# The last tile of an average pool: one load of 64 KB a partition and one whole sum, in place of two column halves

## The chip, the cores and the metric

The kernel runs on one core of a Trainium2 chip. The core has several engines that run side by side and wait for each other through semaphores: TensorE (PE, not used here), VectorE (DVE), ScalarE (ACT), GpSimd (POOL) and SyncE (SP, which here only issues DMAs). Data moves between the chip's HBM and the core's SBUF memory (128 partitions) through 16 DMA engines. The metric is the device time of one execution in microseconds (us); a span, in a profile, is the time from the first to the last event of the program.

## The reference

The input is `x`, float32, of shape 32 x 256 x 4096. Each row of 4096 values is cut into 256 windows of 16 and each window is averaged. The output is 32 x 256 x 256, float32.

```
for i in range(output_size):
    start = int(i * length / output_size)
    end = int((i + 1) * length / output_size)
    result[:, :, i] = np.mean(x[:, :, start:end], axis=-1)
```

So 134.22 MB are read, 8.39 MB are written, and there is about one addition for each value read.

## The kernel before, in words

The 32 x 256 = 8192 rows are cut into 16 tiles of 512 rows. A tile puts four rows (R = 4) on each of the 128 partitions: 4 x 4096 values, 64 KB a partition, 8.39 MB in all. The first fifteen tiles are taken from the first 7680 rows, of which each partition holds 60 in a row, and the last tile (`x_last`, `o_last`) from the last 512 rows. Results of the first fifteen tiles gather in one buffer, `res_many` (60 KB a partition), those of the last in `res_last` (4 KB a partition).

Input tiles come from a pool of two buffers, both named `xin`, so a tile's load waits until the work on the tile two before it has finished with the buffer. All loads are issued by SP, and run in the order of their issue on one DMA queue (q1 in the profile).

`pooled` (L62 to L75) does the work of one stretch of `n` windows, in four instructions:

- POOL (L66) takes the second half of the windows and adds the right 8 values of each onto the left 8, in place;
- VectorE (L69) sums the 16 values of each window of the first half;
- VectorE (L70) sums the 8 values that POOL left of each window of the second half, and so waits for POOL;
- ScalarE (L73) multiplies all `n` results by 1/16, and waits for both sums.

Each engine works through its instructions in the order of the code. In the loop over the first fifteen tiles `pooled` is called once a tile, on 1024 windows a partition. (A clearing of 1536 columns of the second buffer at L80 holds back the second load a little at the start.)

The last tile is handled apart. Its buffer is loaded by two DMAs (L88 to L92), each of half of the columns: 32 KB a partition, 512 windows. Then `pooled` is called on each half. Both halves' results go into `res_last`.

Stores are issued by ScalarE (L57 to L60) and share a second DMA queue (q10), on which they run in the order of issue. There are three: `res_many` in one transfer of 7.86 MB (L93), which stands in the code behind the loads of the last tile and ahead of its work, so that ScalarE issues it after the fifteenth tile's multiplication; and at the end `res_last` in two transfers, of 120 partitions and of 8 (L97). They count on a semaphore of their own, `stored`, for which SP waits at the end (L103).

Of the kernel before, what the change touches and what calls it, by code (L numbers as in the profile page):

```python
# [1 line left out]

# [4 lines left out]


@with_exitstack
def kernel(  # L10
    ctx: ExitStack,
    tc: tile.TileContext,
    x: bass.AP,
    output_size: int,
    out: bass.AP,
):

    nc = tc.nc
    F32 = mybir.dt.float32
    X = mybir.AxisListType.X

    batch, channels, length = x.shape
    ob, oc, olen = out.shape
    assert ob == batch and oc == channels and olen == output_size
    assert length % output_size == 0
    window = length // output_size  # L30
    hw = window // 2
    inv_w = 1.0 / float(window)

    P = nc.NUM_PARTITIONS
    R = 4
    rows = batch * channels
    assert rows % (P * R) == 0
    ntiles = rows // (P * R)
    many = (ntiles - 1) * R
    cells = R * output_size  # L40
    m = cells // 2
    cols = R * length

    xr = x.rearrange("b c l -> (b c) l")
    orow = out.rearrange("b c o -> (b c) o")
    x_many = xr[0 : P * many, :].rearrange("(p r) l -> p (r l)", p=P, r=many)
    o_many = orow[0 : P * many, :].rearrange("(p r) o -> p (r o)", p=P, r=many)
    x_last = xr[P * many :, :].rearrange("(p r) l -> p (r l)", p=P, r=R)
    o_last = orow[P * many :, :].rearrange("(p r) o -> p (r o)", p=P, r=R)

    res_many = nc.alloc_sbuf_tensor("res_many", [P, (ntiles - 1) * cells], F32, align_bytes=256)
    res_last = nc.alloc_sbuf_tensor("res_last", [P, cells], F32, align_bytes=256)
    inpool = ctx.enter_context(tc.tile_pool(name="inpool", bufs=2))

    stored = nc.alloc_semaphore("stored")

    def store(out, in_):  # L57
        ins = nc.scalar.dma_start(out=out, in_=in_)
        tc.no_tile_sem_insts.add(ins.ins.name)
        ins.then_inc(stored, 16)  # L60

    def pooled(xin, res, base, n):  # L62


        k = n // 2
        nc.gpsimd.tensor_add(  # L66
            out=xin[:, k:n, 0:hw], in0=xin[:, k:n, 0:hw], in1=xin[:, k:n, hw:window]
        )
        nc.vector.reduce_sum(out=res[:, base : base + k], in_=xin[:, 0:k, :], axis=X)  # L69
        nc.vector.reduce_sum(  # L70
            out=res[:, base + k : base + n], in_=xin[:, k:n, 0:hw], axis=X
        )
        nc.scalar.mul(  # L73
            out=res[:, base : base + n], in_=res[:, base : base + n], mul=inv_w
        )  # L75

    for t in range(ntiles - 1):
        xbuf = inpool.tile([P, cols], F32, name="xin")
        if t == 1:
            nc.vector.memset(xbuf[:, 0:1536], 0.0)  # L80
        nc.sync.dma_start(out=xbuf, in_=x_many[:, t * cols : (t + 1) * cols])
        pooled(xbuf.rearrange("p (o w) -> p o w", w=window), res_many, t * cells, cells)

    half = cols // 2
    xbuf = inpool.tile([P, cols], F32, name="xin")
    for h in range(2):  # L88
        nc.sync.dma_start(
            out=xbuf[:, h * half : (h + 1) * half],  # L90
            in_=x_last[:, h * half : (h + 1) * half],
        )  # L92
    store(o_many, res_many[:, :])  # L93
    for h in range(2):
        xin = xbuf[:, h * half : (h + 1) * half].rearrange("p (o w) -> p o w", w=window)
        pooled(xin, res_last, h * m, m)
    for lo, hi in ((0, 120), (120, P)):  # L97
        store(o_last[lo:hi, :], res_last[lo:hi, :])

    ctx.pop_all().close()  # L100
    tc.close()
    tc.compile()  # L102
    nc.sync.wait_ge(stored, 48)  # L103
    nc.sync.sem_clear(stored)


# [1 line left out]
_INS = ['x', 'output_size']  # L108
_OUTS = [((32, 256, 256), 'float32')]

_NUMBERS = {'output_size': 256}


# [26 lines left out]
```

## Time and profile before

| | us |
|---|---|
| median of 3 runs | 333.52 (333.38 to 333.53) |
| the profiled execution | 333.36 |
| its span | 332.1 |
| VectorE busy | 211.1 |
| GpSimd busy | 139.9 |
| ScalarE busy | 18.4 |
| DMA: bytes read, written | 134.22 MB, 8.39 MB |
| DMA: mean rate over the span | 429 GB/s |

The profile names an instruction by its line in the code, its engine, its operation and what it writes and reads (`res_many<-xin`), with the shape as partitions x elements. Under "L66", then, stand the POOL additions, under "L69" and "L70" the two sums, under "L73" the multiplications. A line of the timeline gives the start in us from the beginning of the span, the duration, the instruction, and in brackets how long the engine had been idle before it and what ended the wait. "ACTq" and "SPq" are the instructions that issue DMAs. The chain that ended last is read backwards from the program's last work: each step is what released the next one. In the 40-slice row of the DMA engines a 9 means that they were busy for 90% of the slice or more. Below the page, the trace holds a record of each DMA packet (queue, size, start and end); a packet here is what one DMA engine moves for one partition, 65,536 bytes for a whole tile and 32,768 for a half, or the 4-byte write with which it reports that its share of a transfer is done. A transfer over 128 partitions gives each of the 16 DMA engines eight data packets and one such completion write.

### The profile page before, as it was taken

How to read it: one execution, taken by the hardware profiler on the slowest of the kernel's cores; microseconds unless marked ns; L12 is line 12 of the kernel's file. 1: busy time of each engine (PE TensorE's matmuls, PEld its weight loads, DVE VectorE, ACT ScalarE, POOL GpSimd, SP SyncE). 2: the span in 40 equal slices, each digit the busy share in tenths (PEclk: the TensorE clock that was granted, in tenths of full speed). 3: DMA queues.
4: the chain of work that ended last, by engine and by line, in shares of the span. 5: the costliest groups of instructions: out<-in, count | busy, mean ns of one | idle time of the engine just before them, and what ended most of it. 6: DMA issues, size and time to landing. Idle time of an engine off the chain costs nothing.

```text
span 332.1 us, 167 instructions
## 1 busy us (share of the span) xinstructions
DVE 211.1 (64%) x35; ACT 18.4 (6%) x18; POOL 139.9 (42%) x21
## 2 busy tenths in 40 slices
DVE  1029396592939669293966929396693929569770
ACT  1000101001010100101010010101000010100100
POOL 0028091542809154270916427090642709068050
DMA  9898999989898998989899998989899898989997
GB/s 379 379 497 387 482 403 411 474 379 505 379 497 387 458 426 379 505 379 497 387 482 403 395 489 379 505 379 497 387 450 434 379 505 379 497 383 430 442 466 307
DMA packets 2743, 142.61 MB, mean 429 GB/s; under 512 B 311, under 2 KB 311, under 8 KB 439
## 3 DMA queue, kind: packets, MB, share of 16 engines
q1 hardware_dynamic: 2448, 134.22, 93.6%
q10 hardware_dynamic: 295, 8.39, 5.9%
HBM read 134.22 MB, written 8.39 MB: 429 GB/s over the span
## 4 chain that ended last, share of the span: by engine, by line
DMA 62%; POOL 20%; DVE 10%; issue 3%; POOLq 1%; ACT 0%
DMA xin<-in_x_dram 62%; POOL xin L66 20%; DVE res_many L70 9%; POOLq L102 1%; DVE res_last L70 1%; DVE xin L80 0%; ACT res_last L73 0%; POOLq L66 0%
## 5 line engine op out<-in xcount | busy, mean ns | idle before, releaser
L66 POOL TENSOR_TENSOR xin<-xin 128x4096 f32<-128x4096 f32 (+1 forms) x17 | 139.7, 8216 | 179.7 <-DMA xin<-in_x_dram 179.7
L69 DVE TENSOR_REDUCE res_many<-xin 128x512 f32<-128x8192 f32 x15 | 130.3, 8686 | 105.2 <-DMA xin<-in_x_dram 105.2
L70 DVE TENSOR_REDUCE res_many<-xin 128x512 f32<-128x4096 f32 x15 | 66.3, 4419 | 2.4 <-POOL xin L66 2.3
L73 ACT ACTIVATE res_many<-res_many 128x1024 f32<-128x1024 f32 x15 | 15.8, 1056 | 289.9 <-DVE res_many L70 289.9
L69 DVE TENSOR_REDUCE res_last<-xin 128x256 f32<-128x4096 f32 x2 | 8.8, 4414 | 2.1 <-DMA xin<-in_x_dram 2.1
L70 DVE TENSOR_REDUCE res_last<-xin 128x256 f32<-128x2048 f32 x2 | 4.6, 2280 | 0.1
L80 DVE MEMSET xin<- 128x1536 f32 x1 | 1.3, 1338 | 1.1 <-PEq L121 1.1
L73 ACT ACTIVATE res_last<-res_last 128x512 f32<-128x512 f32 x2 | 1.3, 629 | 13.7 <-DVE res_last L70 13.7
L73 ACT ACT_TABLE_LOAD x1 | 1.3, 1283 | 0.7 <-PEq L121 0.7
L121 POOL MEMSET const-float32-0.0<- 128x1 f32 x1 | 0.1, 98 | 0.2 <-issue 0.2
L121 POOL MEMSET const-bfloat16-1.0<- 128x1 bf16 x1 | 0.1, 101 | 0.0
L121 POOL MEMSET const-uint8-127<- 128x1 uint8 x1 | 0.1, 101 | 0.0
L121 POOL MEMSET const-float32-1.0<- 128x1 f32 x1 | 0.1, 98 | 0.0
## 6 DMA issues: line engine op xcount, KB each, us to landing
xin<-in_x_dram SPq DMA_DIRECT2D x2, 4096.0 KB, 21.6
out_dram<-res_many ACTq DMA_DIRECT2D x1, 7680.0 KB
out_dram<-res_last ACTq DMA_DIRECT2D x1, 480.0 KB
xin<-in_x_dram SPq DMA_DIRECT2D x15, 25.3
out_dram<-res_last ACTq DMA_DIRECT2D x1, 32.0 KB
```

The lines of the kernel that those rows point to most:

```text
L66: nc.gpsimd.tensor_add(out=xin[:, k:n, 0:hw], in0=xin[:, k:n, 0:hw], in1=xin[:, k:n, hw:window])
L69: nc.vector.reduce_sum(out=res[:, base : base + k], in_=xin[:, 0:k, :], axis=X)
L70: nc.vector.reduce_sum(out=res[:, base + k : base + n], in_=xin[:, k:n, 0:hw], axis=X)
L73: nc.scalar.mul(out=res[:, base : base + n], in_=res[:, base : base + n], mul=inv_w)
L80: nc.vector.memset(xbuf[:, 0:1536], 0.0)
L102: tc.compile()
L121: nc = _bacc.Bacc("TRN2", target_bir_lowering=False, num_devices=1)
```

## The change

The two DMAs of the last tile become one, of 64 KB a partition, and `pooled` is called once on the whole tile, 1024 windows a partition, as for the other fifteen. The constant `m` goes, since nothing uses it any more. Stores are as before, in the same order.

```
-    m = cells // 2
...
-    half = cols // 2
     xbuf = inpool.tile([P, cols], F32, name="xin")
-    for h in range(2):
-        nc.sync.dma_start(
-            out=xbuf[:, h * half : (h + 1) * half],
-            in_=x_last[:, h * half : (h + 1) * half],
-        )
+    nc.sync.dma_start(out=xbuf, in_=x_last)
     store(o_many, res_many[:, :])
-    for h in range(2):
-        xin = xbuf[:, h * half : (h + 1) * half].rearrange("p (o w) -> p o w", w=window)
-        pooled(xin, res_last, h * m, m)
+    pooled(xbuf.rearrange("p (o w) -> p o w", w=window), res_last, 0, cells)
     for lo, hi in ((0, 120), (120, P)):
         store(o_last[lo:hi, :], res_last[lo:hi, :])
```

On the engines the instructions of the last tile fall from two to one for the load, from two to one for POOL's addition, from four to two for VectorE's sums and from two to one for ScalarE's multiplication, each of twice the size. All other instructions stand in the same order as before.

## The prediction

> **What bounds the kernel now.** I read the page's totals first, then the chain that ended last, then the last 40 us of the timeline, and last the trace's packet records, which give start and end of every DMA packet. Their clock was laid on the timeline's by the last reduction (319.81 us).
>
> ```profile
> DVE 211.1 (64%) x35; ACT 18.4 (6%) x18; POOL 139.9 (42%) x21
> ...
> DMA  9898999989898998989899998989899898989997
> q1 hardware_dynamic: 2448, 134.22, 93.6%
> q10 hardware_dynamic: 295, 8.39, 5.9%
> ```
>
> The 16 DMA engines are busy in every slice, 99.5% over the two queues (q1 loads, q10 stores), while VectorE is busy 64% of the span. Bytes set the time: a compute change costs only where it leaves the DMA engines without work. That can only be at the end, so I look there.
>
> ```profile
> 307.68 7.61 issue
> 315.28 4.50 POOLq L102
> 319.78 0.02 issue
> 319.81 2.30 DVE res_last L70
> 322.10 0.02 issue
> 322.12 0.63 ACT res_last L73
> ```
>
> The chain stops at 322.75, though the span is 332.06: what follows is stores. That the chain runs through compute here doesn't make compute the bound. The timeline shows what lies beside it:
>
> ```profile
> 293.38 8.69 DVE L69 TENSOR_REDUCE res_many<-xin 128x512 f32<-128x8192 f32 x1 [6.04 <-DMA xin<-in_x_dram]
> 293.49 8.72 POOL L66 TENSOR_TENSOR xin<-xin 128x4096 f32<-128x4096 f32 x1 [10.60 <-DMA xin<-in_x_dram]
> 302.24 4.42 DVE L70 TENSOR_REDUCE res_many<-xin 128x512 f32<-128x4096 f32 x1 [0.17 <-POOL xin L66]
> ...
> 306.69 1.06 ACT L73 ACTIVATE res_many<-res_many 128x1024 f32<-128x1024 f32 x1 [18.26 <-DVE res_many L70]
> 307.78 0.38 ACTq L58 DMA_DIRECT2D out_dram<-res_many  x1
> ...
> 315.27 4.42 DVE L69 TENSOR_REDUCE res_last<-xin 128x256 f32<-128x4096 f32 x1 [2.10 <-DMA xin<-in_x_dram]
> 315.32 4.45 POOL L66 TENSOR_TENSOR xin<-xin 128x2048 f32<-128x2048 f32 x1 [7.64 <-DMA xin<-in_x_dram]
> ...
> 322.78 1.04 ACTq L58 DMA_DIRECT2D out_dram<-res_last  x2
> ```
>
> The big store (7.86 MB) is issued at 307.78, the last half lands at 315.27, the small stores (0.52 MB) are issued from 322.78 on the same queue. The packet records tell the rest. The last load's data packets end at 311.9 to 312.6 on the 16 engines. On 15 of them a 61,440-byte packet of the big store (2.27 us) comes next, and the load's 4-byte completion write only behind it, at 314.2 to 314.9: that is why the half lands at 315.27. The big store's packets end at 330.03 to 330.35 on those 15 engines (330.73 on the sixteenth), and the small stores' 4 KB packets follow without a gap to 331.60; the last completion comes at 332.02.
>
> ```profile
> 322.80:330.00 7.20, 0.00 (x0) 0.00 (x0) 0.00 (x0) 1.00 0.94 410
> 330.00:332.06 2.06, 0.00 (x0) 0.00 (x0) 0.00 (x0) 1.00 0.63 255
> ```
>
> In these windows (columns: length, DVE, ACT, POOL busy, clock, DMA share, GB/s) no engine computes for 9 us, and the DMA engines work at 0.94 until 330. So the small stores sit in their queue from 322.78 to 330.03, 7.25 us: that slack is what the change draws on.
>
> **The change, part by part.**
>
> Issue and transfer. SP issues one DMA for two, 0.33 us for 0.81 us, both at 287.37 behind the same wait, with 5 us of the tile before still to land: hidden, worth nothing. The bytes are the same; eight packets of 64 KB an engine (2.417 us each) stand for sixteen of 32 KB (1.213 each), 19.34 for 19.41 us: -0.07 us. The earlier landing of the first half (303.1) is gone.
>
> Work taken away before 315 us. POOL's add at 303.22, DVE's 4.41 + 2.27 from 306.57 and ACT's 0.63 at 313.21 vanish from under the transfer. Nothing waits for them but the second half's work, which started at the landing. On ACT the order stays: fifteenth multiply, big store, then the last tile's multiply; so the big store is issued at 307.78 as before.
>
> Landing. Queue states at 311.9 to 312.6 are the same except for packet size, so I keep 315.27. The bounds: 313.0 if the completion write goes first (312.62 + 0.38 from write to landing), 317.5 if one more store packet (2.27) gets in.
>
> Work after the landing. This is now a whole tile, for which the fifteenth tile is the template: landing 293.38, POOL 8.72, reduction from 302.24, ACT at 306.69, a store issued right behind at 307.78. Landing to issue is 14.40 us. In halves it was 315.27 to 322.78, 7.51. So the small stores are issued at 315.27 + 14.40 = 329.67, 6.89 us later. POOL's add alone is 8.72 - 4.45 = 4.27 of it, the second reduction 4.42 - 2.29 = 2.13, ACT 0.43; rounding and hand-over are the rest. DVE's first reduction (8.69 for 4.42) stays beside POOL's.
>
> What hides it. 6.89 us against 7.25 us in the queue looks free, but an issue isn't a packet. How long an engine takes from issue to useful work on an idle queue, the trace shows once: the first load, issued at 0.74, has its first packets start at 1.73 to 2.42 (0.99 to 1.68 later) and end 1.47 to 2.52 later than issue plus the steady 2.42, median 1.9. The other row is the big store, whose first packet starts 4.13 us after issue, but behind load packets. The engines are idle by 330.4 here, so the first load is nearest; a transfer over 15 engines ends with a late one, so I take 2.0, with 1.0 and 4.1 as ends.
>
> The sum: 329.67 + 2.0 + 8 packets of 0.16 (1.28) + 0.42 (last packet 331.60 to last completion 332.02) + 0.04 to the end of the span = 333.41, against 332.06: **+1.35 us**. The second small store is issued 0.43 later and has one packet an engine (0.16) behind the first's eight: covered. With 1.0 us it is +0.35, with 4.13 us +3.5.
>
> The Trainium skill (DMA: Bandwidth & Descriptors, Latency and other measured facts) states about 600 ns to the first byte on this kind of queue; by that figure packets could start at 330.27, as the big store ends, and the sum would be about 332.0, no change. No engine of the first load did it in under 0.99.
>
> **The base.** The profiled execution took 333.36 us with a span of 332.1; the median of the runs shown is 333.52, 0.16 above. I add the difference to the median: 333.52 + 1.35 = 334.9, rounded down to 334.8 for the 0.07 of the packets. Within 0.2% (0.67 us) is what a measurement can't tell from no change.
>
> **The rivals.**
>
> 1. No change: the completion write goes ahead of the store. For it: the big store was issued at 307.78; with the first load's 0.99 to 1.68 it was ready by 308.8 to 309.5, yet each engine ran one or two more 32 KB packets (from 309.3 and 310.6) before the store's. So an engine seems to pick work ahead. If it does so by number of packets, then with 64 KB packets the completion write is picked before the store is there. Against: picked by bytes or time, the order stays, and one engine of 16 behind a store packet is enough. Price: landing 313.0, issue 327.4, first packet by 329.9 even at 2.5 us, before 330.03: hidden, 333.5. It decides from a landing below about 313.7. The Trainium skill (same page, Queues, rings and completion order) says that an engine drains a whole packet of about 9 to 17 descriptors from one ring before it switches; a share of eight data descriptors and one completion write would then not be broken, and this rival would be the forecast. The trace disagrees on 15 of 16 engines, with a store packet between the eighth and the completion. Chance 0.26.
>
> 2. No change though the landing stays: the small stores start within 1.0 us. +0.35, 333.8. For it: the first load's fastest engine; against: 15 of its 16 ended their first packet 1.66 or more late. Chance 0.07.
>
> 3. Slower still: the store's first packet gets in before the load's eighth, landing 317.5, or the start takes the 4.1 of the big store: +3.5, 337.0. Against the first: at 309.3 to 310.0 every engine took a load packet. Chance 0.06.
>
> That two packets' worth of overhead make it faster: the 0.07 and what the dropped instructions free come nowhere near 0.67. Chance 0.02.
>
> **How the numbers follow.** The forecast (landing kept, start between 1.3 and 2.8 us, +0.7 to +2.1) has 0.59; its own range is 334.2 to 335.7. Slower: 0.59 + 0.06 = 0.65; same: 0.26 + 0.07 = 0.33; faster 0.02. The range takes in rival 1 down to 333.3 and reaches to 335.9, leaving out rival 3 and the far end of the start.
>
> **What would show it.** In the profile after: POOL's sixteenth add near 315.3 with 8.7 us, the last reduction to about 328.5, the small stores' issue near 329.7, and a gap in the DMA engines between 330.4 and 331.7. A first reduction near 313 means rival 1. I'm wrong if the landing moves by 2 us or the store starts much faster or slower than 2 us.

## The result, and the profile after

The changed kernel takes 334.49 us (median of 8 runs, 334.25 to 334.81); the kernel before, beside it, 333.49 us (333.35 to 333.62). The ratio is 1.003, with a 95% interval of 1.0020 to 1.0041: slower by 1.0 us, between 0.7 and 1.4. The forecast was 334.8 and slower by 1.3.

The profiled execution took 334.56 us with a span of 333.2. First its page (totals, queues):

```profile
span 333.2 us, 162 instructions
...
DVE 211.0 (63%) x33; ACT 18.2 (5%) x17; POOL 139.7 (42%) x20
...
DMA  9898989989898989999898989899898989899997
...
q1 hardware_dynamic: 2304, 134.22, 93.2%
q10 hardware_dynamic: 295, 8.39, 6.0%
```

The work is the same to 0.1 to 0.2 us on each engine, and so are the bytes; q1 has 144 records fewer, since the last load has half as many data packets and completion writes. Nothing that is added up here shows where 1 us went. The timeline of the end does:

```profile
293.11 8.69 DVE L68 TENSOR_REDUCE res_many<-xin 128x512 f32<-128x8192 f32 x1 [6.03 <-DMA xin<-in_x_dram]
...
307.51 0.38 ACTq L57 DMA_DIRECT2D out_dram<-res_many  x1
314.90 8.69 DVE L68 TENSOR_REDUCE res_last<-xin 128x512 f32<-128x8192 f32 x1 [8.50 <-DMA xin<-in_x_dram]
315.01 8.72 POOL L65 TENSOR_TENSOR xin<-xin 128x4096 f32<-128x4096 f32 x1 [13.07 <-DMA xin<-in_x_dram]
323.76 4.42 DVE L69 TENSOR_REDUCE res_last<-xin 128x512 f32<-128x4096 f32 x1 [0.18 <-POOL xin L65]
328.21 1.06 ACT L72 ACTIVATE res_last<-res_last 128x1024 f32<-128x1024 f32 x1 [20.73 <-DVE res_last L69]
329.30 0.90 ACTq L57 DMA_DIRECT2D out_dram<-res_last  x2
```

(Line numbers are one to eight lower than before, because lines have gone.) This execution is 0.27 us ahead of the one of before already at the fifteenth tile (293.11 against 293.38). The last tile lands at 314.90 (315.27 before), and the small stores are issued 14.40 us later, at 329.30 (322.78 before). The end of the chain says the same: one wait of 27.76 us for the load, then the tile's work end to end (the piece called `POOLq L94` covers POOL's addition).

```profile
287.11 27.76 DMA xin<-in_x_dram
...
314.98 8.76 POOLq L94
...
323.76 4.43 DVE res_last L69
...
328.21 1.06 ACT res_last L72
```

The packet records show the rest. The big store's packets end at 329.93 to 330.35, nearly as before. The first 4 KB packets of the small stores start at 330.13, 0.83 us after the issue, but 51 of the 128, nearly all of them among the first 64, take more than 0.2 us, about 0.3 on average, where all took 0.159 before. The last one ends at 332.85 (331.60 before), and the last completion comes at 333.21 (332.02). Windows over that second show it (the columns are length, busy DVE, ACT and POOL with their counts, clock, DMA share, GB/s); first the kernel before, then the changed one:

```profile
330.00:331.00 1.00, 0.00 (x0) 0.00 (x0) 0.00 (x0) 1.00 0.85 348
331.00:332.00 1.00, 0.00 (x0) 0.00 (x0) 0.00 (x0) 1.00 0.44 176
```

```profile
330.00:331.00 1.00, 0.00 (x0) 0.00 (x0) 0.00 (x0) 1.00 0.76 172
331.00:332.00 1.00, 0.00 (x0) 0.00 (x0) 0.00 (x0) 1.00 0.86 279
332.00:333.20 1.20, 0.00 (x0) 0.00 (x0) 0.00 (x0) 1.00 0.16 62
```

In the first microsecond after the big store the DMA engines move half of what they moved before, and so the small stores run on into 332 and 333.

### The profile page after: what moved, and what is told of

Its sections match the earlier page's. It is cut to its first block, busy times and chain, and to the rows that moved or that the text cites. A ratio compares the mean times of both kernels' runs of the same rounds, so it can differ in the third digit from the quotient of the medians.

```text
span 333.2 us, 162 instructions
## 1 busy us (share of the span) xinstructions
DVE 211.0 (63%) x33; ACT 18.2 (5%) x17; POOL 139.7 (42%) x20
## 4 chain that ended last, share of the span: by engine, by line
DMA 66%; POOL 18%; DVE 11%; POOLq 3%; issue 0%; ACT 0%
DMA xin<-in_x_dram 66%; POOL xin L65 18%; DVE res_many L69 9%; POOLq L94 3%; DVE res_last L69 1%; DVE xin L79 0%; ACT res_last L72 0%; POOLq L65 0%
## 5 line engine op out<-in xcount | busy, mean ns | idle before, releaser
L65 POOL TENSOR_TENSOR xin<-xin 128x4096 f32<-128x4096 f32 x16 | 139.5, 8717 | 183.8 <-DMA xin<-in_x_dram 183.8
L68 DVE TENSOR_REDUCE res_last<-xin 128x512 f32<-128x8192 f32 x1 | 8.7, 8686 | 8.5 <-DMA xin<-in_x_dram 8.5
L69 DVE TENSOR_REDUCE res_last<-xin 128x512 f32<-128x4096 f32 x1 | 4.4, 4419 | 0.2 <-POOL xin L65 0.2
L72 ACT ACTIVATE res_last<-res_last 128x1024 f32<-128x1024 f32 x1 | 1.1, 1056 | 20.7 <-DVE res_last L69 20.7
```

What stands on the lines that cost most here:

```text
L65: nc.gpsimd.tensor_add(out=xin[:, k:n, 0:hw], in0=xin[:, k:n, 0:hw], in1=xin[:, k:n, hw:window])
L69: nc.vector.reduce_sum(out=res[:, base + k : base + n], in_=xin[:, k:n, 0:hw], axis=X)
L72: nc.scalar.mul(out=res[:, base : base + n], in_=res[:, base : base + n], mul=inv_w)
```

## The experiments

My theory: all the loss is the later issue of the small stores. That issue comes 14.40 us after a landing which itself waits behind a packet of the big store, and it costs only as far as it comes too late to be hidden by the big store. Rivals: the 64 KB transfer costs something by itself; the whole sums do; or the late landing isn't due to the store's packet.

**One part at a time: one load, two sums.** The kernel before, with the new load only:

```
-    for h in range(2):
-        nc.sync.dma_start(
-            out=xbuf[:, h * half : (h + 1) * half],
-            in_=x_last[:, h * half : (h + 1) * half],
-        )
+    nc.sync.dma_start(out=xbuf, in_=x_last)
```

> The load of the last tile is one transfer of 64 KB a partition, the sums stay in two halves. My theory (the loss is the later issue of the small stores, and comes from all data landing at once): landing near 315 as in both kernels, then VectorE works 4.41 + 2.27 + 4.41 + 2.27 = 13.4 us and ScalarE 0.63, so the small stores are issued 14.1 to 14.2 us after the landing, about 0.2 us sooner than in the changed kernel (14.40), and the time is 334.2 to 334.5. Rival (the long sums at the end make the loss, not the load): with halves summed the time is that of before, 333.5.

Measured: 334.27 us, ratio 1.0027 (1.0017 to 1.0036). Landing 314.96, issue 329.05, 14.09 us later:

```profile
314.96 4.42 DVE L69 TENSOR_REDUCE res_last<-xin 128x256 f32<-128x4096 f32 x1 [8.51 <-DMA xin<-in_x_dram]
...
329.05 0.90 ACTq L58 DMA_DIRECT2D out_dram<-res_last  x2
```

The sums in halves don't help once the data comes in one piece: the rival falls.

**The other part alone: two loads, one sum.**

```
-    for h in range(2):
-        xin = xbuf[:, h * half : (h + 1) * half].rearrange("p (o w) -> p o w", w=window)
-        pooled(xin, res_last, h * m, m)
+    pooled(xbuf.rearrange("p (o w) -> p o w", w=window), res_last, 0, cells)
```

> The load stays in two column halves, the sum is whole. My theory: the second half lands near 315.2, the whole sum starts only then, the small stores are issued 14.40 us later, and the time is that of the changed kernel, 334.4 to 334.6. Rival (the 64 KB packets or the lost early landing cost something by themselves on the DMA engines): with the old transfers the time goes back towards 333.5, at most 334.0.

Measured: 334.47 us, ratio 1.0034 (1.0021 to 1.0048), the time of the changed kernel. Its timeline has a turn that I hadn't thought of:

```profile
306.45 8.68 DVE L69 TENSOR_REDUCE res_last<-xin 128x512 f32<-128x8192 f32 x1
...
315.22 8.72 POOL L66 TENSOR_TENSOR xin<-xin 128x4096 f32<-128x4096 f32 x1 [13.15 <-DVE res_last L69]
323.98 4.42 DVE L70 TENSOR_REDUCE res_last<-xin 128x512 f32<-128x4096 f32 x1 [8.86 <-POOL xin L66]
...
329.51 0.91 ACTq L58 DMA_DIRECT2D out_dram<-res_last  x2
```

VectorE's first sum reads only the first half of the columns, and so it starts at 306.45, long before the second half is there. It gains nothing: POOL's windows are all in the second half, and its 8.72 us plus 4.42 and 1.06 are the path. (The trace names VectorE as what released POOL, but that sum, over at 315.13, reads other columns and stands behind POOL's addition in the code. The load's last completion is counted at 315.09, 0.13 us before POOL starts, and in the changed kernel it is 0.14: so POOL waited for the landing.) So the old transfers alone don't bring the time back, and the new one alone is enough to lose it. What counts is how much work stands between the last landing and the stores; either part of the change puts some 14 us there in place of 7.5.

**The same late issue without the change.** The kernel before, with extra multiplications by 1.0 on ScalarE ahead of the small stores, four in one run and six in the other:

```
+    for _ in range(4):
+        nc.scalar.mul(out=res_last[:, :], in_=res_last[:, :], mul=1.0)
     for lo, hi in ((0, 120), (120, P)):
         store(o_last[lo:hi, :], res_last[lo:hi, :])
```

> The kernel before, with four multiplications by 1.0 of all of the last results (1.06 us each) between ScalarE's last multiplication and the small stores, so that these are issued 4.3 us later, near 327.1, with nothing else changed. My theory: the small stores wait in their queue for the big store to 330.0 in any case: no change, 333.4 to 333.6. Rival (what is issued later ends later): +4.3 us, 337.8; or a part of it.

> The kernel before with six such multiplications: the small stores are issued 6.5 us later, near 329.3 to 329.5, which is where the changed kernel issues them. My theory: the same loss as the change, 334.2 to 334.7, with the first small packets near 330.2 to 330.4 and taking about 0.3 us each at first, where they took 0.16 us before. Rival (the change's loss comes from its transfer or its landing): 333.5.

Measured with four: 333.41 us, ratio 0.9998 (0.9990 to 1.0007). With six: 334.39 us, ratio 1.0027 (1.0018 to 1.0037). The ends of the two timelines:

```profile
322.43 4.32 ACT L98 ACTIVATE res_last<-res_last 128x1024 f32<-128x1024 f32 x4
326.77 1.06 ACTq L58 DMA_DIRECT2D out_dram<-res_last  x2
```

```profile
322.98 6.50 ACT L98 ACTIVATE res_last<-res_last 128x1024 f32<-128x1024 f32 x6
329.51 0.91 ACTq L58 DMA_DIRECT2D out_dram<-res_last  x2
```

Some four microseconds more on the chain that ended last (4.3 in multiplications) cost nothing; six and a half cost 0.9 us. With the load, the sums and the landing as before, a late issue alone gives the loss of the change. In the run with six, the first small packets start at 330.35 and mostly take 0.3 us or more each, as in the changed kernel; in the run with four they follow the big store without a gap (329.92) and take 0.159. From issue to last completion it is 3.60 us in the run with six, 3.58 with two loads and one sum, 3.67 with one load and two sums, 3.91 in the changed kernel's profile. Small stores that simply follow the big store are complete at 332.0, as before the change. With 3.6, an issue later than about 332.0 - 3.6 = 328.4 should cost, one earlier not; the issues at 326.77 (four multiplications) and 329.05 (one load, two sums) lie on either side of it.

**What the landing waits for.** The changed kernel, with the big store issued by SP, so that it runs on the queue of the loads and behind them:

```
-    def store(out, in_):
-        ins = nc.scalar.dma_start(out=out, in_=in_)
+    def store(out, in_, eng=nc.scalar):
+        ins = eng.dma_start(out=out, in_=in_)
...
-    store(o_many, res_many[:, :])
+    store(o_many, res_many[:, :], nc.sync)
```

> The changed kernel with the big store issued by SP, on the queue of the loads, so that no packet of it can get ahead of the last load's completion write. My theory: landing near 312.6 instead of 314.9, small stores issued near 327.0, over 3 us before the big store ends near 330.1, so their start is hidden again: 333.4 to 333.7, as before the change. Rival (the last tile's work costs its time wherever it begins, or the stores' bytes bound it otherwise): 334.5 as in the changed kernel.

Measured: 333.47 us, ratio 0.9997 (0.9988 to 1.0006). The loss is gone with the whole load and the whole sums left as they are.

```profile
293.11 8.69 DVE L68 TENSOR_REDUCE res_many<-xin 128x512 f32<-128x8192 f32 x1 [6.04 <-DMA xin<-in_x_dram]
...
307.50 0.34 SPq L57 DMA_DIRECT2D out_dram<-res_many  x1
312.99 8.69 DVE L68 TENSOR_REDUCE res_last<-xin 128x512 f32<-128x8192 f32 x1 [6.60 <-DMA xin<-in_x_dram]
...
327.39 3.15 ACTq L57 DMA_DIRECT2D out_dram<-res_last  x2
```

The last tile lands at 312.99, 1.91 us sooner, with the fifteenth tile's landing at the same 293.11. The packet records have the order: data to 312.06 to 312.60, then the 4-byte completion write at once, then the store's first packet. In the changed kernel the store's packet (2.267 us) stands between the two on every one of the 16 engines. The gain is less than 2.27 because the last load packets end 0.25 to 0.37 us later here. The small stores, issued at 327.39, start when the big store ends, at 330.17.

**A shorter packet in the way: 4 KB.** The big store cut into 4 KB a partition and 56 KB:

```
-    store(o_many, res_many[:, :])
+    store(o_many[:, 0:cells], res_many[:, 0:cells])
+    store(o_many[:, cells:], res_many[:, cells:])
```

> The changed kernel with the big store cut in two transfers on the same queue, 4 KB a partition first and 56 KB then, so that the store packet ahead of the completion write takes 0.16 us and not 2.27. My theory: landing near 312.9, small stores issued near 327.3, time 333.4 to 333.7. Rival (the completion is late for another reason, such as the store's traffic as a whole, or several small packets get in): landing stays at 314 to 315, time 334.2 to 334.6.

Measured: 335.49 us, ratio 1.0065 (1.0053 to 1.0078), a miss of both. The first part holds only the first tile's results and was issued as soon as these were there, at 37.05 us, into the midst of the loads; a packet of 57,344 bytes (2.116 us) of the second part stood ahead of the completion writes. So it says nothing on the packet's length, but something else:

```profile
294.46 8.69 DVE L68 TENSOR_REDUCE res_many<-xin 128x512 f32<-128x8192 f32 x1 [6.08 <-DMA xin<-in_x_dram]
...
316.08 8.69 DVE L68 TENSOR_REDUCE res_last<-xin 128x512 f32<-128x8192 f32 x1 [8.34 <-DMA xin<-in_x_dram]
...
330.49 0.93 ACTq L57 DMA_DIRECT2D out_dram<-res_last  x2
```

The 0.52 MB moved in among the loads puts the later landings back by about 1.2 us (the fifteenth tile's is at 294.46 for 293.11, and 0.13 us of that stood already at the first tile's). The sum of the bytes is the same, and the time is 1.0 us longer than the changed kernel's: the end now hangs on the last landing, and what delays that is passed on.

The packet records of this run also show how the two queues share an engine. From 41.07 to 61.65 us, on all 16 engines, the 4 KB store packets and the packets of the loads take turns, one each. Where the second tile's load ends among them, on 15 engines its last data packet is followed by a store packet and only then by the completion write. At the end of the program it is the same order with a longer store packet.

**A shorter packet, put right: 1 KB.** Both parts now need the fifteenth tile:

```
-    store(o_many, res_many[:, :])
+    edge = many * output_size - 256
+    store(o_many[:, edge:], res_many[:, edge:])
+    store(o_many[:, :edge], res_many[:, :edge])
```

> The changed kernel with the big store cut so that both parts need the fifteenth tile: 1 KB a partition first, 59 KB then, on the same queue and issued one behind the other near 307.5. (The run with 4 KB first had its first part issued at 37 us, because it held only the first tile's results, and so did not do this.) My theory: the engines choose packet by packet between the two queues, so only a 1 KB packet (about 0.04 us) or a few of them get ahead of the last load's completion writes: landing 312.3 to 313.0, small stores issued 326.7 to 327.4, under the 328.4 from which they cost, time 333.3 to 333.7. Rival (what holds up the completion is the store's start as such, not the length of its packet): landing near 314.9 and 334.5.

Measured: 334.68 us, ratio 1.0035 (1.0021 to 1.0049). The landing is as my theory has it, the time is not:

```profile
307.81 4.74 ACTq L57 DMA_DIRECT2D out_dram<-res_many  x2
312.81 8.69 DVE L68 TENSOR_REDUCE res_last<-xin 128x512 f32<-128x8192 f32 x1 [6.12 <-DMA xin<-in_x_dram]
...
327.21 1.66 ACTq L57 DMA_DIRECT2D out_dram<-res_last  x2
```

The last tile lands at 312.81 and the small stores are issued at 327.21. What takes the gain is a new wait: the second part's issue is held on ScalarE from 308.23 for 4.31 us (an issue took 0.28 to 0.62 us in nearly all other places), until the first part's packets run, so that the 59 KB packets start at 313.05 and not at 311.8. The DMA engines stand idle for about 1 us or less before it, and the store ends at 330.91 to 331.39, not at 329.93 to 330.35. The small packets follow without a gap, but many of the first ones are slow here too (0.25 to 0.5 us), and the last completion comes at 333.53. So this run shows that the length of the store's packet sets the landing (on 13 of the 16 engines one 1 KB packet stands between data and completion write, on three none), and loses the time in another place.

**Small stores on idle engines.** The changed kernel with the big store cut down to `o_many[:, 0:256]`:

> The changed kernel with the big store cut down to 1 KB a partition: 59 of the 60 KB of results a partition aren't stored, so the time is that of a kernel with 7.7 MB less to write. It shows how small stores start on idle engines. My theory: landing near 312.5, issue near 326.9, first packets 0.8 to 1.0 us later, 4 KB packets of 0.3 us at first, the last completion 3.2 to 3.6 us after the issue: span near 330.3. Rival (the slow first packets of the changed kernel come from the end of the big store beside them): packets of 0.16 us from the first on, last completion about 2.6 us after the issue.

One execution, 332.59 us, span 331.3, where 330.3 was expected: landing and issue came 0.75 us later than expected, and nearly all of that stood already at the fifteenth tile's landing (293.85 for 293.11 in the changed kernel). The 1 KB was issued at 37.22, since it too holds only the first tile's results, and its packets took turns with the loads' until 60.96. The small stores' issue is at 327.65, the first packets start 0.84 us later, most packets take 0.3 to 0.45 us at first and 0.159 from about the sixtieth of the 128, and the last completion comes 3.59 us after the issue. No big store was near: the slow first packets belong to the start of these stores, not to the end of the other. Landing was 313.25, with the last load's data ended at 312.88 on the latest engine: without a store packet in the way, 0.37 us.

## Why the prediction was right

*The bound and the place.* Right. The bytes and the engines' work were unchanged, and the whole difference lies behind 330 us.

*Landing kept.* Right: 314.90, or 315.17 with the 0.27 us added by which this execution was ahead, against 315.27 predicted. Rival 1 (the completion write goes first) had 0.26. On none of the 16 engines did it come true, so the engines don't pick ahead by a number of packets in the way that it needed; with packets twice as long, the store's still came in between, and its first packet started 4.30 us after the issue, where it had been 4.13. The Trainium skill (DMA: Bandwidth & Descriptors, Queues, rings and completion order) has engines drain typically about 9 to 17 descriptors of one ring before they switch; the traces don't agree, as the switch came between the eighth data packet and the completion write behind it, and in the run with 4 KB first, load and store packets took turns one by one on all 16 engines.

*Landing to issue.* 14.40 us predicted from the fifteenth tile, 14.40 measured.

*What hides it.* Right in kind: 6.89 us of delay was more than the small stores could take. The queue time of 7.25 us less the 2.0 taken for the start left 5.25; the run with four multiplications and the one with one load and two sums put the limit between 4.0 and 6.3 us of delay (326.77 and 329.05, against 322.78); by the estimate from the 3.6 us it is 5.6.

*The start of the small stores.* The sum was nearly right, its parts were not. Predicted: 2.0 us to useful work, then 8 packets of 0.16 and 0.42 to the last completion, together 3.70. Measured: 0.83 us to the first packet, then 2.7 us of packets, of which most in the first half take about twice the time, then 0.36; 3.91 together in this profile, 3.58 to 3.67 in five of the other runs. By the prediction's own measure (the end of an engine's first packet, less the steady time) the start took about 1 us on most engines, and not 2.0; and a start much faster than 2 us was one of its signs of being wrong. The gap in the DMA engines that it expected between 330.4 and 331.7 isn't there either: they work at 0.76 and 0.86 in those two microseconds, on slow packets. The start taken too long and the packets taken too fast cancel, and that they do so this closely is luck. The first load's row stood for a slow beginning; whether it is the same slowness isn't shown. Rival 2 (start within 1.0 us, no change) had the start right, but not that packets would be slow. The Trainium skill (the same page, Anatomy of one DMA) gives a fit of about 2.0 us plus the bytes over 436 GB/s, made for DMAs issued by GpSimd; for 0.52 MB that would be an estimate of 3.2 us, and these stores, issued by ScalarE, took 3.6.

*The sum.* +1.35 in the profile, against +1.19 measured (333.25 against 332.06): the head start took off 0.27 and the landing 0.10, and the small stores, with 3.91 for 3.70, gave back 0.21. The median moved by 1.0, and the interval reaches to 1.4.

## What to carry to other kernels

When a kernel is bound by its bytes, the tail of the last tile is free only as long as another transfer covers it: compare the last issue, plus what a fresh store needs (3.6 us for 0.52 MB here), with the time at which that store would be complete if it only queued behind the covering transfer (332.0 here, some 1.7 us after the big store's end), before taking time out of or putting time into the chain that ended last. A large store that starts on another queue just as the last load ends can put one of its packets ahead of that load's completion, and the length of the packet is the price; the store issued behind the load on the load's own queue paid nothing, and with it the simple whole-tile tail was as fast as the halves. How a tile is cut matters at the end by what the last landing releases: half a load helps only if the work on it is half too.

## What the runs showed of the hardware that was not expected

- 4 KB store packets that follow the big store without a break took 0.159 us each in the kernel before, in the run with four multiplications and, but for one of 0.21, in the one with the big store on SP's queue. Stores issued about 1 us before the big store's end or later began with packets of about 0.3 us, some 0.45. How early the issue comes isn't the whole of it: in the run with 1 KB first they were slow although issued 3.7 us before the big store's end, and in the one with the big store on SP's queue fast at 2.8 us. What makes them slow stays open.
- An issue can be held. ScalarE's second store in a row took 4.31 us in the run with 1 KB first and 2.50 us in the run with the big store on SP's queue (0.28 to 0.62 us in nearly all other places); in both, the first store's packets had not begun when the second was issued, and the hold ended when they were running. That alone can't be the cause: in the kernel before and in the run with four multiplications the first small store's packets had not begun either (330.02 and 329.92), and the second issue took 0.43 and 0.44 us. There the big store was running on ScalarE's own queue; in the two runs with a hold, no earlier store was running on it, and the engines were busy with the other queue's packets. Whether that makes the difference was not tried.
